# Expert weights in pages of 8 KB a partition, a contraction order to match, and a last normalization with two-row products

## The chip, the cores and the metric

The kernel runs on one core of a Trainium2 chip. The metric is the device time of one execution in microseconds (us), from the first to the last instruction and what the runtime lays around them. The engines have names of their own in the profile: PE is TensorE (its weight loads stand apart as PEld), DVE is VectorE, ACT is ScalarE, POOL is GpSimd, and SP is SyncE, which here issues nearly all transfers.

## What is computed

One block of a diffusion transformer over 512 latent tokens of 1024 channels, with 256 context tokens. First an attention half (a latent attention of 8 heads beside a differential attention of 4), then an expert half, each followed by a residual and a layer norm. The change touches both halves, the second most:

```python
def ec_moe(h, w_router, b_router, w1, w3, w2):
    cap = EC_CAPACITY * n // N_EXPERTS                       # 64 tokens an expert
    aff = softmax((h @ w_router + b_router), axis=-1)
    g, idx = top_k(swapaxes(aff, 1, 2), cap)                 # each of 16 experts takes 64 tokens
    xe = h[bidx, idx]
    hid = silu(einsum('becd,edf->becf', xe, w1)) * einsum('becd,edf->becf', xe, w3)
    ye = einsum('becf,efd->becd', hid, w2) * g[..., None]
    return zeros_like(h).at[bidx, idx].add(ye)

x = layer_norm(ALPHA * x + g2 * ec_moe(x * (1 + sc2) + sh2, ...), ln2_g, ln2_b)
```

Each expert has three matrices of 1024 x 1024 in float32, 12.6 MB; sixteen experts are 201 MB.

## The kernel before

Tokens lie on 128 partitions in NT = 4 tiles. The attention half multiplies the tokens with w_in in blocks of columns. Each block has four pieces of weights: a piece is loaded raw (`w_load`, L192), split into a high and a low part (`w_piece`, L198; ACT makes the high part, DVE the low one), and multiplied in three products (`mm3`, L79). The pages for that are the N_WS = 6 buffers of `wpage` (L128), 4 KB a partition each. Beside these products run the sums over w_ada (`mod_chunk`, L334), whose loads share SP's queue. The same small pages hold a part of the softmax (L758) and the weights of the branch outputs (`wo_load`, L789); the output projection has pages of its own (`page`, N_PG = 18, and `page2`, N_PG2 = 9).

The expert half works on pairs of experts (the loop at L1232). For a pair it gathers the tokens by products with one-hot matrices (`gather`, L1122), multiplies with w1 and w3 (`up_`, L1164), transposes (`hid_t`, L1179), multiplies with w2 (`down`, L1185), and puts the result back into the accumulators `acc` by one-hot products (`scatter`, L1193), half of it inside the next pair's `up_`. PE's instructions run in the written order there (`manual_schedule`, L1228).

The weights come through a ring of pages. `order` (L920) lists all pieces of 128 rows in the order of use; `prefetch` (L947) issues them on SP, each into the next of N_RING = 36 pages (L928), and SP waits there until the page is free. Nine pieces (`places`, L926) go into tiles that are not in use yet (`hold`, L944). A piece is 512 KB: 128 partitions with one row of 4 KB each. The contraction index of partition p in piece k is 128 k + p, and the activations that meet the weights are cut in the same way.

At the end the last pair's w2 is taken in three parts of columns (PARTS, L40: first column, width, rows in a page). `put` (L1278) scales and splits a part's product at once, and the function that it returns puts it back and takes statistics; that one is called after the first piece of the next part (L1310). The last part is accumulated in PSUM (`fin`). After it come the mean and variance, and for each tile two DVE passes over 768 columns (L1335, L1336); ACT and POOL do the last 256 columns (L1325 to L1331). The rows ln2_g and ln2_b are loaded as broadcasts behind the last weights (L1265).

## Time and profile before

| | |
|---|---|
| median of 3 runs | 1049.84 us (1048.28 to 1052.63) |
| the profiled execution | 1047.56 us |
| its span, first to last instruction | 1045.8 us |
| PE busy | 977.7 us, 93% of the span |
| PEld, DVE, ACT, POOL busy | 614.1, 451.9, 278.2, 176.1 us |
| moved by DMA | 266.97 MB, mean 255 GB/s |
| the chain that ended last | PE 72%, DMA 16%, DVE 7% |

The profile shows one execution. Busy shares are means over stages with different limits, so the stages are read one by one: the span cut into 40 slices, tables of stretches with the busy time of each engine, the granted clock of TensorE (1.00 is 2.4 GHz, 0.50 is 1.2 GHz), the share of time in which the 16 DMA engines had packets, and what they moved; then lists of who waited for whom; then the chain of work that ended last. A line number such as L1174 is that of the kernel's source.

### The profile page before, as it was taken

What the parts mean: (1) busy time and instruction counts of PE and PEld (TensorE: products, weight loads), DVE (VectorE), ACT (ScalarE), POOL (GpSimd) and SP (SyncE); (2) the same over time, 40 slices, a digit from 0 to 9 for tenths busy, and PEclk for the clock granted to TensorE, in tenths of its full rate; (3) what the DMA queues carried; (4) which work ended last, traced back from release to release, by engine and by line L of the source; (5) the groups of instructions that cost most, each with busy time, mean ns of one, the idle gap of its engine ahead of it and who ended that gap; (6) DMA issues with size and microseconds to landing.
All of it is one profiled execution on the core that took longest, in us unless ns stands there. A gap on an engine that the chain in (4) does not pass through costs nothing.

```text
span 1045.8 us, 13799 instructions
## 1 busy us (share of the span) xinstructions
PE 977.7 (93%) x5266; PEld 614.1 (59%) x5266; DVE 451.9 (43%) x870; ACT 278.2 (27%) x556; POOL 176.1 (17%) x177
## 2 busy tenths in 40 slices
PE   6999998989999999999986999999999999999992
PEld 5888976768778777777754443535353534334331
DVE  2382365753678556648473512221313131111227
ACT  1222324224777555544120101010101010010010
POOL 2340020202577422210020500000000000000004
PEclk9999999999999999999997999999999999999996
DMA  9944347763012000028948979999999999999993
GB/s 297 290 152 136 97 115 247 232 201 82 21 39 58 22 19 22 21 82 295 411 167 321 371 300 409 409 409 409 409 410 409 408 410 407 410 409 409 409 372 115
DMA packets 101209, 266.97 MB, mean 255 GB/s; under 512 B 14020, under 2 KB 37528, under 8 KB 101144
## 3 DMA queue, kind: packets, MB, share of 16 engines
q1 hardware_dynamic: 100248, 264.52, 68.3%
q0 software_dynamic: 320, 1.05, 0.4%
q8 instruction: 41, 0.67, 0.3%
q10 hardware_dynamic: 576, 0.52, 0.1%
q14 instruction: 24, 0.20, 0.1%
HBM read 261.47 MB, written 2.10 MB: 252 GB/s over the span
## 4 chain that ended last, share of the span: by engine, by line
PE 72%; DMA 16%; DVE 7%; ACT 2%; issue 2%; POOL 2%; SPq 0%; DVEq 0%; ACTq 0%; POOLq 0%
PE h L1174 16%; DMA wr<-moe_w 10%; PE y L1190 9%; PE mx L1137 6%; PE acc L83 5%; PE acc L82 5%; PE acc L81 5%; PE sc L652 4%; PE tpb L660 3%; DMA wa<-w_ada 3%; PE av L840 3%; PE mx L1203 2%; DMA wraw<-w_in 2%; PE tp L236 2%; PE po L83 1%
## 5 line engine op out<-in xcount | busy, mean ns | idle before, releaser
L1174 PE MATMUL h<-wr,xe 128*64 128x512 f32 x1024 | 233.6, 598 | 8.7 <-DMA wr<-moe_w 7.2
L1174 PEld LDWEIGHTS h<-wr,xe 128*64 128x64 f32 x1024 | 68.3, 136 | 162.9 <-issue 106.6
L1190 PE MATMUL y<-wr,hidT 128*64 128x512 f32 x448 | 97.7, 594 | 0.0
L641 DVE TENSOR_REDUCE nm<-sc 128x1 f32<-128x768 f32 x64 | 61.0, 953 | 34.3 <-PE sc L652 33.8
L1177 DVE TENSOR_TENSOR hid<-hid,h 128x512 f32<-128x512 f32 x16 | 11.0, 687 | 145.2 <-PE h L1174 145.2
L1149 POOL TENSOR_TENSOR oh<-oh,aff 128x512 f32<-128x512 f32 x8 | 8.4, 1048 | 352.8 <-PE mx L1137 352.8
L1190 PEld LDWEIGHTS y<-wr,hidT 128*64 128x64 f32 x448 | 31.5, 137 | 61.8 <-issue 58.1
L642 ACT ACTIVATE P<-sc,nm 128x768 f32<-128x768 f32 x64 | 57.6, 901 | 31.8 <-DVE nm L641 22.7
L1137 PE MATMUL mx<-oh,xn 128*128 128x128 f32 x512 | 60.3, 279 | 1.4 <-DVE oh L1127 1.4
L1137 PEld LDWEIGHTS mx<-oh,xn 128*128 128x128 f32 x512 | 59.2, 196 | 2.5 <-issue 1.3
L74 ACT ACTIVATE whi<-wraw 128x1024 fp32r<-128x1024 f32 (+1 forms) x32 | 33.5, 1046 | 99.4 <-DMA wraw<-w_in 75.4
L77 DVE TENSOR_TENSOR wlo<-wraw,whi 128x1024 fp32r<-128x1024 f32 (+1 forms) x32 | 39.2, 1227 | 45.2 <-PE acc L82 29.7
L74 ACT ACTIVATE ye<-y 128x512 fp32r<-128x512 f32 (+2 forms) x17 | 9.7, 572 | 178.8 <-DVE y L1197 98.7
L81 PE MATMUL acc<-xlh,whi 128*128 128x512 f32 x128 | 51.5, 402 | 2.1 <-ACT whi L74 2.1
L1204 DVE TENSOR_TENSOR acc<-acc,mx 128x512 f32<-128x512 f32 x56 | 34.7, 680 | 41.4 <-PE mx L1203 41.4
L1176 ACT ACTIVATE hid<-h 128x512 f32<-128x512 f32 x16 | 9.6, 597 | 155.6 <-PE h L1174 155.6
L82 PE MATMUL acc<-xll,whi 128*128 128x512 f32 x128 | 50.7, 396 | 0.0
L83 PE MATMUL acc<-xlh,wlo 128*128 128x512 f32 x128 | 50.2, 401 | 0.3 <-DVE wlo L77 0.3
L81 PE MATMUL acc<-whi,xlh 128*128 128x512 f32 (+1 forms) x128 | 49.6, 391 | 1.0 <-ACT whi L74 1.0
L1197 DVE SCALAR_TENSOR_TENSOR y<-y,gate,g2b 128x512 f32<-128x512 f32 x14 | 9.9, 754 | 92.5 <-PE y L1190 92.5
L83 PE MATMUL acc<-whi,xll 128*128 128x512 f32 (+1 forms) x128 | 48.7, 381 | 0.5 <-POOL xll L77 0.5
L82 PE MATMUL acc<-wlo,xlh 128*128 128x512 f32 (+1 forms) x128 | 48.8, 381 | 0.2 <-DVE wlo L77 0.2
(339 smaller groups left out, 1707.3 us busy)
## 6 DMA issues: line engine op xcount, KB each, us to landing
wr<-moe_w SPq DMA_DIRECT2D x372, 512.0 KB, 10.2
wa<-w_ada SPq DMA_DIRECT2D x32, 512.0 KB, 4.3
wraw<-w_in SPq DMA_DIRECT2D x28, 512.0 KB, 5.2
wa<-w_ada SPq DMA_DIRECT2D x8, 1024.0 KB, 9.4
wr<-moe_w SPq DMA_DIRECT2D x16, 384.0 KB, 8.5
outraw<-w_out SPq DMA_DIRECT2D x8, 512.0 KB, 9.6
xq<-x SPq DMA_DIRECT2D x4, 512.0 KB, 8.2
q<-q SPq DMA_DIRECT2D x16, 128.0 KB, 2.3
```

The source lines that it names most:

```text
L74: S.activation(hi, src, AF.Copy)
L77: (eng_lo or V).tensor_tensor(lo, src, f(hi), op=OP.subtract)
L81: T.matmul(ps, lh, rh, start=start, stop=False)
L82: T.matmul(ps, lh, rl, start=False, stop=False)
L83: T.matmul(ps, ll, rh, start=False, stop=stop)
L641: V.tensor_reduce(nm, ps[:, :768], axis=AX.X, op=OP.max, negate=True)
L642: S.activation(p, ps[:, :768], AF.Exp, bias=nm, accum_out=z)
L652: T.matmul(ps[:, a:b], l, r[:, a:b], start=i == 0, stop=i == len(passes) - 1)
L1137: T.matmul(pss[hf][:, kk * 128:(kk + 1) * 128], xn[t][:, k * 128:(k + 1) * 128], o[:, t].rearrange("p e s -> p (e s)"), start=t == 0, stop ...
L1174: T.matmul(ph[i][64 * hf:64 * hf + 64, :], xe[:, k, sl], w[:, hf * 512:(hf + 1) * 512], start=k == 0, stop=k == KD - 1)
L1190: T.matmul(py[hf][r0:r0 + 64, :], hT[:, e % 2, fc % 4, fc // 4, :], w[:, hf * 512:(hf + 1) * 512], start=fc == 0, stop=fc == KD - 1)
L1204: V.tensor_tensor(acc[t][:, hs], acc[t][:, hs], ps, op=OP.add)
```

## The change

Pages are 8 KB a partition, [128, 2, 1024], and half as many: 3, 9, 4 and 2. The contraction index of the experts is cut as (k p i) with i of two: partition p holds rows 256 k + 2 p and 256 k + 2 p + 1 of a matrix, which follow one another in HBM, and a transfer is 1 MB. What meets these weights takes every second column (`chan`): the gather's xn, the transposes of hid and of xn, and the vectors and router weights that belong to channels. In the attention half a page holds two raw pieces (`halves_`) or a high and a low part. The held pieces are pairs of halves of four pages.

At the end, `put` is called whole as soon as a part's product is there. Parts 0 and 1 are multiplied by ln2_g then (part 0 on DVE, part 1 on POOL). After the statistics, minus mean over deviation and a row of ones are transposed into two rows, and a product of these with the two rows ln2_g, ln2_b gives the term that a single DVE pass adds. The rows of ln2 are loaded on ACT's queue at the end of the last but one pair, into xn.

Left out below are the same edits in `rows_use`, `latent`, `mod_end` and `page`.

```diff
-N_WS, N_PG, N_PG2, N_PG3, N_P, N_WA = 6, 18, 9, 3, 5, 3
+N_WS, N_PG, N_PG2, N_PG3, N_P, N_WA = 3, 9, 4, 2, 5, 3
...
-PARTS = (0, 384, 2), (384, 384, 2), (768, 256, 4)
+PARTS = (0, 384, 4), (384, 384, 4), (768, 256, 8)
...
-    def wpage(name, dt=F32, shape=None):
-        return ws.tile(shape or [128, 2, 512], dt, name=name, tag="ws", bufs=N_WS)
+    def wpage(name, dt=F32):
+        return ws.tile([128, 2, D], dt, name=name, tag="ws", bufs=N_WS)
+    pairs = {}
+    def halves_(key, page_, name, dt=F32):
+        if key in pairs:
+            return pairs.pop(key)[:, 1]
+        pairs[key] = page_(name, dt)
+        return pairs[key][:, 0]
+    def chan(k):
+        return slice(256 * (k // 2) + k % 2, 256 * (k // 2) + 256, 2)
...
         if (col, kk) not in raws:
-            raws[col, kk] = wpage("wraw")
+            raws[col, kk] = halves_("wraw", wpage, "wraw").rearrange("p (k n) -> p k n", k=2)
             dma(raws[col, kk][:, :, :n], w_in[:, 2 * kk:2 * kk + 2, col:col + n])
...
         raw = w_load(col, n, kk)
-        hi = wpage("whi", F32R)
-        lo = wpage("wlo", F32R)
+        hi, lo = (wpage_[:, i].rearrange("p (k n) -> p k n", k=2) for wpage_ in (wpage("whl", F32R),) for i in range(2))
         split(hi[:, :, :n], lo[:, :, :n], raw[:, :, :n])
...
-    dma(wrt, A["moe_w_router"][0].rearrange("(k p) e -> p k e", p=128))
+    dma(wrt.rearrange("p (k i) e -> p k i e", i=2), A["moe_w_router"][0].rearrange("(k p i) e -> p k i e", p=128, i=2))
...
-                                       wpage("P1", F32, [128, D])[:, :768] if m else p_tile()))
+                                       halves_("P1", wpage, "P1")[:, :768] if m else p_tile()))
...
-        raw = page_("oraw", F32, [128, 4, 256])
+        raw = halves_("oraw", page_, "oraw").rearrange("p (k n) -> p k n", k=4)
...
-        hi = page_("ohi", F32R, [128, 4, 256])
-        lo = page_("olo", F32R, [128, 4, 256])
-        split(hi, lo, raw)
-        return hi, lo
+        hl = page_("ohl", F32R).rearrange("p i (k n) -> p i k n", k=4)
+        split(hl[:, 0], hl[:, 1], raw)
+        return hl[:, 0], hl[:, 1]
...
-        raw = page("outraw", F32, [128, 2, 512])
+        raw = halves_("outraw", page, "outraw").rearrange("p (k n) -> p k n", k=2)
...
-        woh[hf].append(page_("woh", F32R, [128, 2, 512]))
-        wol[hf].append(page_("wol", F32R, [128, 2, 512]))
+        hl = page_("wohl", F32R).rearrange("p i (k n) -> p i k n", k=2)
+        woh[hf].append(hl[:, 0])
+        wol[hf].append(hl[:, 1])
...
-    def page2(name, dt=F32, shape=None):
-        return Q2.tile(shape or [128, D], dt, name=name, tag="pg2", bufs=N_PG2)
-    wsrc = {n: A["moe_" + n][0].rearrange("e (k p) n -> e p k n", p=128) for n in ("w1", "w3", "w2")}
+    def page2(name, dt=F32):
+        return Q2.tile([128, 2, D], dt, name=name, tag="pg2", bufs=N_PG2)
+    wsrc = {n: A["moe_" + n][0].rearrange("e (k p i) n -> e p k i n", p=128, i=2) for n in ("w1", "w3", "w2")}
...
-             for k in range(KD) for n in ns]
-    order[-2 * KD:] = [(E_N - 2 + i, "w2", (q, kh)) for q, p in enumerate(PARTS) for kh in range(KD // p[2]) for i in range(2)]
+             for k in range(KD // 2) for n in ns]
+    order[-KD:] = [(E_N - 2 + i, "w2", (q, kh)) for q, p in enumerate(PARTS) for kh in range(KD // p[2]) for i in range(2)]
...
-    places = {2: "gb", 5: "ye", 8: "acc0", 10: "acc1", 12: "acc2", 13: "hid", 16: "acc3", 21: "ohT", 27: "hidT"}
+    places = {2: ("gb", "acc0"), 8: ("acc1", "acc2"), 10: ("acc3", "ye"), 12: ("ohT", "hidT")}
...
             c0, w, ks = PARTS[q]
-            dma(t[:, :ks * w].rearrange("p (k n) -> p k n", k=ks), wsrc[nm][e, :, ks * kh:ks * kh + ks, c0:c0 + w])
-        else:
-            dma(t, wsrc[nm][e, :, k, :])
-        loaded[e, nm, k] = t
+            t = t.rearrange("p i d -> p (i d)")[:, :ks * w].rearrange("p (k i n) -> p k i n", i=2, n=w)
+            for a in range(ks // 2):
+                dma(t[:, a], wsrc[nm][e, :, ks // 2 * kh + a, :, c0:c0 + w])
+            loaded[e, nm, k] = t
+            return
+        dma(t, wsrc[nm][e, :, k])
+        for j in range(2):
+            loaded[e, nm, 2 * k + j] = t[:, j]
...
     def hold(nm):
-        load(next(i for i in places if places[i] == nm), place(nm).tile([128, D], F32, name="wr", tag=nm, bufs=1))
+        i, j = next((i, j) for i in places for j in range(2) if places[i][j] == nm)
+        e, n, k = order[i]
+        t = place(nm).tile([128, D], F32, name="wr", tag=nm, bufs=1)
+        dma(t, wsrc[n][e, :, k, j])
+        loaded[e, n, 2 * k + j] = t
...
-            load(order_r[r], page_("wr", F32, [128, D]))
+            load(order_r[r], page_("wr"))
...
-                T.transpose(ps[:, k * 128:(k + 1) * 128], xn[t][:, (4 * hf + k) * 128:(4 * hf + k + 1) * 128], ident)
+                T.transpose(ps[:, k * 128:(k + 1) * 128], xn[t][:, chan(4 * hf + k)], ident)
...
-    def page3(name, dt=F32, shape=None):
-        return rM2.tile(shape or [128, D], dt, name=name, tag="pg3", bufs=N_PG3)
+    def page3(name, dt=F32):
+        return rM2.tile([128, 2, D], dt, name=name, tag="pg3", bufs=N_PG3)
...
-    for nm in ("ye", "hid", "ohT", "hidT"):
+    for nm in ("ye", "ohT", "hidT"):
...
-                T.matmul(pss[hf][:, kk * 128:(kk + 1) * 128], xn[t][:, k * 128:(k + 1) * 128],
+                T.matmul(pss[hf][:, kk * 128:(kk + 1) * 128], xn[t][:, chan(k)],
...
-            T.transpose(ps[:, j * 128:(j + 1) * 128], hid[:, i, j * 128:(j + 1) * 128], ident)
+            T.transpose(ps[:, j * 128:(j + 1) * 128], hid[:, i, chan(j)], ident)
...
         waiting = py, ohT, gt
+        if pr == E_N // 2 - 2:
+
+            lng, lnb, gbr = xn[1], xn[2], xn[0][0:2]
+            for i, nm in enumerate(("ln2_g", "ln2_b")):
+                S.dma_start(xn[1 + i], A[nm].to_broadcast([128, D]))
+                S.dma_start(xn[0][i:i + 1], A[nm])
     prefetch(len(order_r))
-    ln2 = []
-    for nm, place in (("ln2_g", "xe"), ("ln2_b", "hid")):
-        b = me.tile([128, D], F32, name="ln2", tag=place, bufs=1)
-        dma(b, A[nm].to_broadcast([128, D]))
-        ln2.append(b)
-    lng, lnb = ln2
     nb = D // BN_W
...
                     V.bn_stats(bs[:, t, (c0 + b) // BN_W, :], r[:, b:b + BN_W])
+                if not last:
+                    (G if q else V).tensor_tensor(r, r, lng[:, qs_], op=OP.mult)
         return rest
-    rest = None
+    mrs = me.tile([128, NT, 2], F32, name="mrs")
+    V.memset(mrs[:, :, 1], 1.0)
     for q, (c0, w, ks) in enumerate(PARTS):
...
         for kh in range(KD // ks):
-            wp = [piece(E_N - 2 + i, "w2", (q, kh))[:, :ks * w].rearrange("p (k n) -> p k n", k=ks) for i in range(2)]
+            wp = [piece(E_N - 2 + i, "w2", (q, kh)) for i in range(2)]
             for kk in range(ks):
...
                 for i in range(2):
-                    T.matmul(py[64 * i:64 * i + 64, :w], hT[:, i, fc % 4, fc // 4, :], wp[i][:, kk, :],
+                    T.matmul(py[64 * i:64 * i + 64, :w], hT[:, i, fc % 4, fc // 4, :], wp[i][:, kk // 2, kk % 2, :],
                              start=fc == 0, stop=fc == KD - 1)
-            if rest:
-                rest()
-                rest = None
-        rest = put(q, py)
-    rest()
-    order_.close()
+        put(q, py)()
     ov = out[0].rearrange("(t p) d -> p t d", p=128)
     mv = me.tile([128, NT, 2], F32, name="mv2")
-    rs2 = me.tile([128, 2, NT], F32, name="rs2")
+    rs2 = me.tile([128, NT], F32, name="rs2")
     for t in range(NT):
         V.bn_aggr(mv[:, t, :], bs[:, t])
-    G.tensor_scalar(rs2[:, 0, :], mv[:, :, 1], 1.0, EPS / ALPHA ** 2, op0=OP.mult, op1=OP.add)
-    G.tensor_tensor(rs2[:, 0, :], rs2[:, 0, :], negh[:, :NT], op=OP.pow)
-    V.scalar_tensor_tensor(rs2[:, 1, :], mv[:, :, 0], -1.0, rs2[:, 0, :], op0=OP.mult, op1=OP.mult)
+    V.tensor_scalar(rs2, mv[:, :, 1], EPS / ALPHA ** 2, None, op0=OP.add)
+    G.tensor_tensor(rs2, rs2, negh[:, :NT], op=OP.pow)
+    V.scalar_tensor_tensor(mrs[:, :, 0], mv[:, :, 0], -1.0, rs2, op0=OP.mult, op1=OP.mult)
+
+    mt = psd.tile([128, 512], F32, name="mx", bufs=3)
     for t in range(NT):
-        S.activation(acc[t][:, c0:], fin[t], AF.Identity, scale=rs2[:, 0, t:t + 1], bias=rs2[:, 1, t:t + 1])
-    done = []
+        T.transpose(mt[0:2, t * 128:(t + 1) * 128], mrs[:, t, :], ident)
+    mr = me.tile([2, 512], F32, name="mr", tag="hid", bufs=1)
+    V.tensor_copy(mr, mt[0:2])
+
+    for t in range(NT):
+        S.activation(acc[t][:, c0:], fin[t], AF.Identity, scale=rs2[:, t:t + 1], bias=mrs[:, t, 0:1])
+        G.tensor_tensor(acc[t][:, c0:], acc[t][:, c0:], lng[:, c0:], op=OP.mult)
+        G.tensor_tensor(acc[t][:, c0:], acc[t][:, c0:], lnb[:, c0:], op=OP.add)
+        S.dma_start(ov[:, t, c0:], acc[t][:, c0:])
     for t in range(NT):
         o = acc[t]
-        G.tensor_tensor(o[:, c0:], o[:, c0:], lng[:, c0:], op=OP.mult)
-        G.tensor_tensor(o[:, c0:], o[:, c0:], lnb[:, c0:], op=OP.add)
-        S.dma_start(ov[:, t, c0:], o[:, c0:])
-        parts = [slice(0, c0)] if t < NT - 1 else [slice(0, c0 // 2), slice(c0 // 2, c0)]
-        for p in parts:
-            with tc.issue_after(done[-1].ins) if t > 1 else nullcontext():
-                V.scalar_tensor_tensor(o[:, p], o[:, p], mv[:, t, 0:1], lng[:, p], op0=OP.subtract, op1=OP.mult)
-            done.append(V.scalar_tensor_tensor(o[:, p], o[:, p], rs2[:, 0, t:t + 1], lnb[:, p], op0=OP.mult, op1=OP.add))
-            dma(ov[:, t, p], o[:, p])
+        for a, b in ((0, 512), (512, c0)):
+            w = psd.tile([128, 512], F32, name="y" if a else "mx", bufs=2 if a else 3)
+            T.matmul(w[:, :b - a], mr[:, t * 128:(t + 1) * 128], gbr[:, a:b], start=True, stop=True)
+            V.scalar_tensor_tensor(o[:, a:b], o[:, a:b], rs2[:, t:t + 1], w[:, :b - a], op0=OP.mult, op1=OP.add)
+            if t == NT - 1:
+                dma(ov[:, t, a:b], o[:, a:b])
+        if t < NT - 1:
+            dma(ov[:, t, :c0], o[:, :c0])
+    order_.close()
```

## Rows read from the trace of the kernel before

**Rows 1.** The page, part 2: 40 slices of the span, busy tenths and GB/s.

```profile
PE   6999998989999999999986999999999999999992
...
GB/s 297 290 152 136 97 115 247 232 201 82 21 39 58 22 19 22 21 82 295 411 167 321 371 300 409 409 409 409 409 410 409 408 410 407 410 409 409 409 372 115
```

**Rows 2.** Stretches: length, busy us of each engine, PEclk, DMA share, GB/s.

```profile
613.00:865.00 252.00, 252.00 (x1288) 110.63 (x1284) 61.79 (x116) 28.35 (x57) 4.20 (x4) 1.00 1.03 408
865.00:1000.00 135.00, 127.36 (x611) 48.30 (x608) 25.58 (x49) 11.00 (x21) 2.10 (x2) 1.00 1.03 408
1000.00:1012.00 12.00, 11.33 (x59) 5.73 (x57) 2.23 (x5) 1.69 (x3) 0.00 (x0) 1.00 1.06 372
1015.00:1018.00 3.00, 2.86 (x16) 1.05 (x12) 1.39 (x5) 0.00 (x0) 0.00 (x0) 1.00 1.10 351
600.00:613.00 13.00, 13.00 (x83) 8.15 (x84) 2.73 (x8) 2.17 (x4) 1.05 (x1) 1.00 0.57 205
```

**Rows 3.** Waits from 865 to 1000 us: total us, times, longest.

```profile
PEld h L1174 <- DMA wr<-moe_w: 43.8, 47, 1.1
```

**Rows 4.** The chain in order of time: start us, us, what.

```profile
662.48 13.88 PE y L1190 x64
...
709.67 7.15 PE mx L1137 x64
717.25 13.88 PE y L1190 x64
```

**Rows 5.** Queues and DMA issues: packets, MB, share; KB each, us to landing.

```profile
q8 instruction: 41, 0.67, 0.3%
...
wr<-moe_w SPq DMA_DIRECT2D x372, 512.0 KB, 10.2
...
ln<-ln_g SPq DMA_DIRECT2D x1, 512.0 KB, 8.7
```

**Rows 6.** The tile wraw: duration ns min/median/max, and us from issue to landing.

```profile
L74 ACT ACTIVATE whi<-wraw x32: 897/1060/1325, 15.9 to 253.0; 128x1024 fp32r<-128x1024 f32 x28, 128x832 fp32r<-128x832 f32 x4
L77 DVE TENSOR_TENSOR wlo<-wraw,whi x32: 1017/1224/1829, 17.5 to 254.4; 128x1024 fp32r<-128x1024 f32 x28, 128x832 fp32r<-128x832 f32 x4
...
DMA to landing us min/median/max: 3.4/4.8/8.7
```

**Rows 7.** Stretches of ten us in the projections, columns as in rows 2.

```profile
170.00:180.00 10.00, 7.09 (x26) 4.16 (x25) 5.45 (x6) 6.45 (x28) 0.00 (x0) 0.83 0.61 196
...
210.00:220.00 10.00, 7.88 (x27) 5.78 (x25) 4.99 (x4) 2.57 (x3) 0.00 (x0) 0.83 0.69 226
```

**Rows 8.** Groups by line, 600 to 1000 us: busy us, mean ns, idle.

```profile
L1137 PE MATMUL mx<-oh,xn 128*128 128x128 f32 x433 | 49.5, 275 | 0.0
L1137 PEld LDWEIGHTS mx<-oh,xn 128*128 128x128 f32 x432 | 48.8, 192 | 0.0
...
L1197 DVE SCALAR_TENSOR_TENSOR y<-y,gate,g2b 128x512 f32<-128x512 f32 x14 | 9.9, 754 | 92.5 <-PE y L1190 92.5
...
L117 PE MATMUL mx<-rm,one 1*128 1x512 f32 x4 | 1.9, 639 | 0.0
```

**Rows 9.** The chain from 1010 us on: start us, us, what.

```profile
1009.41 9.24 DMA wr<-moe_w
...
1018.70 1.94 PE y L1308 x14
...
1025.50 0.40 DVE y L1283
...
1030.04 0.83 POOL rs L1321
...
1032.11 1.01 DVE acc L1335
...
1041.72 0.96 DVE acc L1336
```

**Rows 10.** Two us of the end, columns as in rows 2.

```profile
1030.00:1032.00 2.00, 0.00 (x0) 0.00 (x0) 0.81 (x1) 0.00 (x0) 1.87 (x2) 0.50 0.00 0
```

More of the change, by code (lines that the diff above doesn't have):

```diff
@@ L168, in _layer @@
     V.tensor_scalar(cs[:, :, 1], sg[:, 8:16], 0.5, None, op0=OP.mult)
-    rows = st.tile([68, 128], F32, name="rows")
+    rows = st.tile([52, 128], F32, name="rows")
+    lnr = st.tile([128, 512], F32, name="xtmp", bufs=3)[:8, :256]
     def rows_load():
@@ L175, in rows_load @@
         dma(rows[51:52], A["diff_g_subln"])
-        dma(rows[52:60], A["ln1_g"][0].rearrange("(k p) -> k p", p=128))
-        dma(rows[60:68], A["ln1_b"][0].rearrange("(k p) -> k p", p=128))
+        for i, nm in enumerate(("ln1_g", "ln1_b")):
+            dma(lnr[4 * i:4 * i + 4], A[nm][0].rearrange("(k p) -> k p", p=256))
     def rows_use():
         tp = psa.tile([128, 512], F32, name="tp", bufs=2)
-        T.transpose(tp[:, :68], rows, ident[:68, :68])
-        V.tensor_copy(vecs[:, 16:84], tp[:, :68])
+        T.transpose(tp[:, :52], rows, ident[:52, :52])
+        for k in range(2):
+            T.transpose(tp[:, 64 + 8 * k:72 + 8 * k], lnr[:, k::2], ident[:8, :8])
+        V.tensor_copy(vecs[:, 16:68], tp[:, :52])
+        for k in range(2):
+            V.tensor_copy(vecs[:, 68 + k:84:2], tp[:, 64 + 8 * k:72 + 8 * k])
         V.tensor_scalar(gsub, vecs[:, 67:68], 1.0 - LAMBDA_INIT, None, op0=OP.mult)
@@ L463, in latent @@
             dma(tq[:, :, i, :], A[nm].rearrange("(t p) d -> p t d", p=128))
-        wukv = wpage("wukv", F32, [128, HEADS, 128])
+        wukv = halves_("wu", wpage, "wu").rearrange("p (h d) -> p h d", d=128)
         dma(wukv, A["mla_w_ukv"][0].rearrange("p (h d) -> p h d", d=128))
@@ L468, in latent @@
         for k in range(2):
-            wuq = wpage("wuq", F32, [128, D])[:, :768]
+            wuq = halves_("wu", wpage, "wu")[:, :768]
             dma(wuq, A["mla_w_uq"][0, k * 128:(k + 1) * 128, :])
@@ L587, in mod_end @@
             for c in range(4):
-                T.transpose(pt[:, c * 128:(c + 1) * 128], rm[i][:, c * 128:(c + 1) * 128], ident)
+                T.transpose(pt[:, c * 128:(c + 1) * 128], rm[i][:, chan(c)], ident)
             ptr.append(pt.rearrange("p (c g o) -> p g c o", g=4, o=32))
@@ L868, in _layer, with page @@
     Q, _ = pool("pages", side="left")
-    def page(name, dt=F32, shape=None):
-        return Q.tile(shape or [128, D], dt, name=name, tag="pg", bufs=N_PG)
+    def page(name, dt=F32):
+        return Q.tile([128, 2, D], dt, name=name, tag="pg", bufs=N_PG)
     yp, close_yp = pool("yp", side="left")
```

## Prediction

> **What bounds the kernel now.** I read the 40 slices first, then tables of stretches, then the waits, the chain in order of time, and the groups by line. In the slices [rows 1] the reader is to see two halves. Up to some 450 us PE is busy and DMA, after the first slices, is not full. From the 25th slice to the 38th, GB/s stands at 407 to 410, whatever PE does. The table [rows 2] says why: 408 GB/s both from 613 to 865 us, where PE never rests, and from 865 to 1000, where it does. So in the expert half the stream of weights runs flat out from 613 us on, and PE catches up with it. The waits [rows 3] show PE on the stream's heels after 865: 47 weight loads waited for a page. The chain [rows 4] gives PE's own pace: 717.25 - 662.48 = 54.8 us a pair of experts. A pair is 48 transfers of 512 KB = 25.2 MB, at 408.5 GB/s 61.6 us. The stream is the slower by 6.8 us a pair; the pages filled beforehand hide that until 865. Just before 613 the ring of pages was full: 205 GB/s from 600 to 613 [rows 2], with PE in the gather and releasing no page. What happens there is set by PE, and what follows by the stream. So three things count: the stream's rate after 613 us, what is put into the stream, and the end behind it. All before 613 counts only where PE stalls.
>
> **The rate.** The same table has three sizes of contiguous row at a full queue [rows 2]: 4 KB rows (613 to 1000) 408, in the slices 409, taken as 408.5 GB/s, 1.5 KB rows (parts of w2, 1000 to 1012) 372, 1 KB rows (1015 to 1018) 351. Over 16 engines that is 160.4, 66.1 and 46.7 ns a row. The line through the first two is 9.5 ns + 0.0368 ns a byte; it gives 47.2 for 1 KB, measured 46.7, so it is a line. An 8 KB row would take 9.5 + 301.8 = 311 ns: 421 GB/s, 3.0% more. In the new layout one partition's two rows of a weight matrix lie one behind the other both in HBM and in the page, so 8 KB can go as one. The trace has no 8 KB row of weights. The bounds are therefore nothing (cut back into 4 KB) and the line. Packets above 4 KB do exist: queue q8 moved 0.67 MB in 41, 16 KB each [rows 5]. I take the line: 387 us x (1 - 408.5/421) = **-11.5 us**, with 0 as the other end. The Trainium skill (DMA: Bandwidth & Descriptors, Why small descriptors are slow) speaks against so much: it has a fixed cost of about 3 cycles a packet, one cycle for each 32 bytes. The rows make it 9.5 ns against 1.18 ns for 32 bytes, some 8. By the page's figure 4 KB to 8 KB would be worth 1.1%, an estimate of -4.4 us; the measured line decides for the sum, and the smaller gain is a rival below.
>
> **What is put into the stream.** Both ln2 rows (512 KB each) used to be issued behind the last weights [rows 5], so they delayed nothing on the path. Now ACT issues them when the last gather has read xn, near 940 us, into the full stream: 1.05 MB / 0.42 = **+2.5 us** (none, if the stream had slack there; rows 1 show none). The two 4 KB rows for the products are nothing beside that.
>
> **Pages of 8 KB.** 36 ring pages of 4 KB become 18 of 8 KB, so as much is filled beforehand. A page is free only when both its halves are used: after the full ring the first release comes one half later, 13.88/16 = **+0.9 us** [rows 4]. Transfers in flight: 10.2 us to landing [rows 5] at 1.28 us each is 8; eight of 1 MB hold more pages, but the bytes landed by a given time, which PE lives on, are the same. The pieces held in other tiles now belong to early, paired halves; PE did not wait there before, so I give nothing.
>
> **The projections.** Six small pages become three, with two raw weights in one page and hi and lo in another. Raw piece 2 of a block can now be loaded only when piece 1 is split, not piece 0. SP issues in order, so the w_ada transfers behind it wait too, and VectorE's sums over them. From the tile's rows [rows 6]: split 1.06 + 1.22, landing 4.8 (worst 8.7), split again 2.3: 9.4 us, against two pieces of 24 matmuls, some 11 us. The slack is 1.6 us; at the worst landing 2.3 us are missing. PE already stalls in two stretches here, 2.9 and 2.1 us idle in ten [rows 7]. Six blocks of this length: 0 to +14 us, and as piece 3 is issued earlier than now, a gain of up to 2 is possible. Landings were near the median, so I take **+1.5 us**.
>
> **Strided loads.** Gather, hid and xn transposes now load weights from every second column. PE's loads take 192 ns and overlap the matmuls, 7.15 us a gather of 64 [rows 4, 8]. No row shows a stationary operand at a step of two. Bounds: nothing, or twice the time (+7.2 us a gather). I take nothing, since the words used are 8 bytes apart; the rival has the price. The Trainium skill (Advanced Engine Details and Errata, Memory Cachelines) wants two hits in a 16-byte line for full speed, and a step of two float32 gives two; no run so far shows it.
>
> **The end.** The last w2 transfer landed about 1018.65 + 2 x 1.49 = 1021.6 us [rows 2, 9]; call it D. Before, part 1 was put back only after half of part 2's product (1020.6 on), and VectorE came to part 2 at 1025.50, D + 3.9. Now part 1 is put back when ready, but PE, in written order, waits for VectorE and ACT (about 1.8 us) and then spends 2.3 on the put, as before, and part 2's product (2 x 1.94) comes after: D + 3.2, so -0.7. The first part's multiplication by gamma (four of 0.5 us) falls between parts; part 1's goes to POOL, idle there. POOL's 0.83 us [rows 9] becomes a small VectorE one: -0.8. Then the old end is two VectorE passes over 768 columns a tile, 1032.11 to 1042.68 = 10.6 us. The new one: transposes 0.8, copy 0.65, then for each tile a two-row product of 512 and of 256 columns, each followed by one VectorE pass (0.75 for 512 columns [rows 8], some 0.45 for 256). A 512-column product of one row took 0.94 us (two instructions, 1.9 for two products) at full clock [rows 8]; the clock here stands at 0.50, that is 1.2 GHz [rows 10], so 1.9. Warm 4 x 1.4 = 5.6, cold 11.3, so 7.5 to 13.2 us with the last pass: -3.1 to +2.6. PE may come warm half way; I take -0.3. Sum for the end **-1.8** (-4.6 to +1.1). The last output transfer stays, 3.1 us.
>
> **Sum.** -11.5 + 2.5 + 0.9 + 1.5 - 1.8 = -8.4 us. The profiled execution took 1047.56 (span 1045.8), so 1039.2 on its scale; the three runs shown have a median of 1049.84, 2.3 above it, and on that scale I forecast **1041.4 us**.
>
> **The rivals.**
> - *The rate stays at 409* (rows cut at 4 KB, or engines at their limit). For it: the share of 1.03 is already called full. Against it: the line through three sizes. -8.4 + 11.5 = +3.1: 1053. Chance 0.13.
> - *Only part of the 9.5 ns is paid per row*, the rest per 4 KB. With a third of it per row, 8 KB takes 2 x 160.4 - 3.2 = 317.6 ns, 412.7 GB/s, -3.9 us instead of -11.5: 1049. For it: no row here is longer than 4 KB. Against: the line holds from 1 to 4 KB. Chance 0.07. The Trainium skill's rule above would come out here.
> - *Slower: strided weight loads.* PE's slack under the faster stream is small: its work without waits ends part 2 at some 1009 us (pair 6's product at 936.5 + 13.9, then 33 of up, 3, 14 of parts and 8 of puts), the stream's at 1016. So from 7 us / (7 x 72 loads) = 14 ns a load, PE becomes the bound. At twice the time: 7.2 for the first gather, 7 x 7.8 for the others, less 7: 1041 + 55 = 1096. For it: no cover in the gather, PE and its loads are both full there [rows 8]. Against: nothing seen. Chance 0.07.
> - *The three pages stall the projections* by the worst landing each time: +14 in place of 1.5: 1053.6. For it: two stretches stall already [rows 7]. Against: DMA has room there, landings were mostly short. Chance 0.08.
>
> **How the numbers follow.** The forecast has 0.65. Half a per cent, 5.2 us, is about what a measurement of this kernel tells from no change. Of the 0.65 I give 0.62 to faster, 0.03 to within 0.5%. Smaller gain: within. Rate unchanged: 0.12 within, 0.01 slower. Pages: 0.04 and 0.04. Strides: 0.07 slower; 0.02 more for slower from the sum of small costs is taken from the within. Faster 0.62, within 0.24, slower 0.14. The likeliest case's own range is 1034 (warm products, no stall) to 1046; for 8 in 10 it goes up to the unchanged rate, 1034 to 1053.
>
> **What would show it.** Right: packets of 8 KB, 420 GB/s or more from 613 us on, the last weights near 1013, PE waiting for pages later than 865 (near 950); the table of the projections no more than 2 us longer before 470; after the last weights some 22 us in place of 24. Wrong: 409 GB/s again with 8 KB pages (rate); weight loads above 200 ns in the gather and a pair longer than 54.8 us (strides); more idle PE from 150 to 240 us with SP waiting for VectorE's split (pages); products at 1.9 us each to the end (clock).

## The result and the profile after

| | median of the runs, us | ratio to before, 95% interval | profiled run: time, span, us |
| --- | --- | --- | --- |
| before | 1049.1 (1045.2 to 1052.6, 6 runs) | 1 | 1047.6, 1045.8 |
| changed | 1056.5 (1055.4 to 1058.6, 6 runs) | 1.0077 [1.0056, 1.0098] | 1055.8, 1053.9 |

The changed kernel is 7.4 us slower; the forecast was 1041.4. Yet the rate of the stream of weights, the term that carried the forecast, came out as worked out. One execution of the run on the places (1419 us) and one of the run on the deferred puts (4803 us) were in a slow state and are in no figure below. The page of the changed kernel, GB/s in 40 slices, answers to [rows 1]:

```profile
GB/s 301 253 174 155 82 125 255 242 187 61 28 33 56 40 1 41 1 160 294 325 152 312 318 284 422 421 421 421 421 421 421 421 420 420 422 421 420 415 286 80
DMA packets 74827, 266.95 MB, mean 253 GB/s; under 512 B 10686, under 2 KB 34058, under 8 KB 51724
```

From the 25th slice on 421 GB/s, where [rows 1] has 409: 311 ns for 8 KB on one of 16 engines, as the line through three row sizes gave. By an estimate from the fixed cost a packet in the Trainium skill (DMA: Bandwidth & Descriptors, Why small descriptors are slow), 1.1% would have come of it. Measured is 2.9%, and the measurement decides.

Stretches of the changed kernel, columns as in [rows 2]:

```profile
613.00:865.00 252.00, 252.00 (x1284) 113.31 (x1285) 58.74 (x112) 27.09 (x53) 7.46 (x7) 1.00 0.98 407
865.00:1000.00 135.00, 129.29 (x650) 56.13 (x646) 29.87 (x56) 13.44 (x27) 2.10 (x2) 1.00 1.01 420
...
700.00:1030.00 330.00, 318.97 (x1624) 143.69 (x1622) 82.56 (x172) 34.29 (x68) 8.12 (x8) 0.99 0.99 406
```

and the last of these for the kernel before:

```profile
700.00:1030.00 330.00, 316.75 (x1600) 135.09 (x1596) 79.66 (x175) 31.65 (x62) 5.25 (x5) 1.00 1.00 396
```

The first row shows where the gain went. From 613 to 865 the mean is 407 GB/s, as before, though the stream runs at 421 once it is full: it became full later. At 700 us the changed kernel had 330 x 406 = 134.0 MB still to move, the one before 330 x 396 = 130.7. The 3.3 MB are 7.8 us of stream at 421, and the rate saves 9.5 us on 130.7 MB (130.7 / 0.4085 less 130.7 / 0.421). Most of the delay stands between the first gather and the first pair's product with w2. In the rows, oh are the one-hot matrices, xe the gathered tokens, which VectorE scales and takes out of PSUM (the evacuation), h the products with w1 and w3, y those with w2. PE in the changed kernel (start us, us, what, and in brackets the idle time before it with its releaser; of y only the start is read, as the window ends there):

```profile
576.66 4.04 PE L1163 MATMUL mx<-oh,xn 128*128 128x128 f32 x32
583.81 20.82 PE L1200 MATMUL h<-wr,xe 128*64 128x512 f32 x96 [3.11 <-DVE xe L1168]
...
606.59 0.74 PE L1163 MATMUL mx<-oh,xn 128*128 128x128 f32 x4 [0.90 <-DVE oh L1153]
608.00 7.33 PE L1163 MATMUL mx<-oh,xn 128*128 128x128 f32 x60 [0.67 <-DVE oh L1153]
...
617.53 0.65 PE L1216 MATMUL y<-wr,hidT 128*64 128x512 f32 x2
```

The same of the kernel before:

```profile
571.70 3.84 PE L1137 MATMUL mx<-oh,xn 128*128 128x128 f32 x32
576.04 20.82 PE L1174 MATMUL h<-wr,xe 128*64 128x512 f32 x96 [0.50 <-DVE xe L1142]
...
607.64 0.65 PE L1190 MATMUL y<-wr,hidT 128*64 128x512 f32 x2
```

The first gather started at 562.57 (before 558.92), the first y at 617.53 (607.64): of 9.9 us, 6.2 arose in between. PE waited 3.11 us for VectorE's evacuation of the gather (xe; before 0.50) and 1.57 us for the next one-hot (before 0.17); 1.3 more lie in the first half of the gather, 6.50 in place of 5.18 us, as the clock rose from 0.50 to 1.00 only near 568 us and not near 561. VectorE at that time, in the changed kernel:

```profile
581.49 0.90 DVE L1242 TENSOR_TENSOR acc<-xn,gb 128x512 f32<-128x512 f32 x1 [10.94 <-PE mx L1163]
582.74 0.69 DVE L1243 TENSOR_TENSOR acc<-acc,gb 128x512 f32<-128x512 f32 x1 [0.36 <-DMA gb<-ln_b]
583.35 1.36 DVE L1168 TENSOR_SCALAR xe<-mx,ghv,bhv 128x128 f32<-128x128 f32 x4
...
605.36 2.59 DVE L1153 TENSOR_TENSOR oh<-iot,slt 128x256 f32<-128x256 f32 x2
```

and in the kernel before:

```profile
575.58 1.37 DVE L1142 TENSOR_SCALAR xe<-mx,ghv,bhv 128x128 f32<-128x128 f32 x4 [9.99 <-PE mx L1137]
577.16 0.69 DVE L1216 TENSOR_TENSOR acc<-xn,gb 128x512 f32<-128x512 f32 x1 [0.22 <-PE h L1174]
...
597.58 0.75 DVE L1127 TENSOR_TENSOR oh<-iot,slt 128x256 f32<-128x256 f32 x2
```

Two instructions of the base sum (`base`: xn times gamma, plus beta) stand ahead of the evacuation that PE waits for. The row blames PE's gather, but that was done at 576.66 + 4.04 = 580.70. The rows of the tile gb, the gamma and beta of the base sum, point to another: POOL issued the load of gamma at 574.8, and the shortest landing is 6.6 us, so it was there at 581.4 at the earliest (worked out, as the trace gives no landing of this one load):

```profile
L1238 POOL DMA_DIRECT2D gb<-ln_g x2: 587/672/757, 574.8 to 597.2; - x2
...
DMA to landing us min/median/max: 6.6/7.4/9.4
```

Before, the issues were at 568.1 and 570.4, with landings as long (6.7 to 9.0). The tiles that the base sum needs hold weights first. gb held w1's second piece and now the third; ye held a piece of the first expert and now one of the second, so the gamma of POOL's half of the base sum is loaded at 597.2 in place of some 570. And in the program before, the planner (which orders each engine's instructions) had put all eight evacuations ahead of the base sum on VectorE.

The one-hot was late for another reason. POOL worked on its half from 604.99 on (before from 578.59 to 591.29), and VectorE's two one-hot instructions beside it took 2.59 us in place of 0.75. So it is in all traces: 2.25 to 2.90 us in the eight with the places of the changed kernel, where POOL's half runs beside them, 0.75 or 0.76 in the other eight, where it was done before.

At the other end, the chain of the changed kernel from the last w1 and w3 on:

```profile
1001.83 2.82 PE h L1200 x12
...
1007.96 5.33 PE y L1337 x32
...
1013.99 0.04 issue
1014.03 0.50 ACT ye L74
1014.56 0.57 DVE ye L77
...
1017.34 5.33 PE y L1337 x32
...
1025.92 1.65 PE mx L1317 x4
1027.57 4.32 PE y L1337 x32
1031.92 0.50 DVE y L1309
...
1036.74 1.05 POOL rs L1346
...
1039.82 2.07 PE mx L1364 x2
1041.89 0.85 PE y L1364 x2
1042.74 1.71 PE mx L1364 x2
```

From 1007.96 on no transfer of weights stands in the chain: PE, not the stream, ends the three parts. It is VectorE's turn for part 2 at 1031.92, where [rows 9] has 1025.50. From the end of the last h product to the end of the span it is 1053.9 - 1004.6 = 49.3 us; before 1045.8 - 999.7 = 46.1 (the last h started at 998.65 and took 1.08). The granted clock in that stretch, columns as in [rows 10]:

```profile
1024.00:1026.00 2.00, 1.32 (x5) 0.74 (x5) 1.24 (x3) 0.19 (x1) 0.00 (x0) 0.88 0.01 4
1026.00:1028.00 2.00, 2.00 (x8) 1.37 (x10) 2.00 (x9) 0.00 (x0) 1.00 (x2) 0.50 0.00 0
...
1040.00:1042.00 2.00, 2.00 (x3) 0.96 (x4) 0.07 (x1) 0.00 (x0) 1.92 (x4) 0.50 0.20 66
1048.00:1050.00 2.00, 2.00 (x4) 0.66 (x2) 0.77 (x2) 0.00 (x0) 0.00 (x0) 0.50 0.43 165
```

It was at 0.50 (1.2 of 2.4 GHz) within the second put, after PE had stood still 1.59 us for ACT. It rose to 1.00 in part 2's product, was at 0.50 again by 1036, while PE stood still for 3.54 us, and stayed there through all two-row products, with PE busy 10.00 us of 10.00 from 1040 to 1050.

### The profile page after: what moved, and what is told of

Same layout as the page of the kernel before. It is cut to its first block, busy times and chain, and to the rows that moved or that the text cites. A ratio compares the mean times of both kernels' runs of the same rounds, so it can differ in the third digit from the quotient of the medians.

```text
span 1053.9 us, 13455 instructions
## 1 busy us (share of the span) xinstructions
PE 989.2 (94%) x5288; PEld 630.4 (60%) x5288; DVE 443.7 (42%) x877; ACT 277.6 (26%) x556; POOL 174.1 (17%) x180
## 4 chain that ended last, share of the span: by engine, by line
PE 73%; DMA 13%; DVE 6%; issue 4%; ACT 2%; POOL 2%; SPq 0%; ACTq 0%; DVEq 0%; POOLq 0%
PE h L1200 16%; PE y L1216 8%; DMA wr<-moe_w 7%; PE mx L1163 5%; PE sc L670 5%; PE acc L83 4%; PE acc L82 4%; PE acc L81 4%; DMA wa<-w_ada 3%; PE tpb L678 3%; PE av L857 3%; PE mx L1229 2%; PE tp L254 1%; PE y L1337 1%; PE av L794 1%
## 5 line engine op out<-in xcount | busy, mean ns | idle before, releaser
L1200 PE MATMUL h<-wr,xe 128*64 128x512 f32 x1024 | 226.1, 594 | 10.7 <-DMA wr<-moe_w 7.1
L1200 PEld LDWEIGHTS h<-wr,xe 128*64 128x64 f32 x1024 | 71.4, 137 | 154.4 <-issue 130.8
L1163 PE MATMUL mx<-oh,xn 128*128 128x128 f32 x512 | 64.8, 289 | 2.8 <-DVE oh L1153 2.8
L1163 PEld LDWEIGHTS mx<-oh,xn 128*128 128x128 f32 x512 | 63.7, 204 | 4.1 <-DVE oh L1153 1.9
L77 DVE TENSOR_TENSOR whl<-wraw,whl 128x1024 fp32r<-128x1024 f32 (+1 forms) x32 | 39.2, 1226 | 56.0 <-ACT whl L74 56.0
L74 ACT ACTIVATE whl<-wraw 128x1024 fp32r<-128x1024 f32 (+1 forms) x32 | 33.2, 1038 | 107.4 <-DMA wraw<-w_in 57.3
L81 PE MATMUL acc<-xlh,whl 128*128 128x512 f32 x128 | 51.0, 399 | 0.0
L83 PE MATMUL acc<-xlh,whl 128*128 128x512 f32 x128 | 50.2, 396 | 0.5 <-DVE whl L77 0.5
L81 PE MATMUL acc<-whl,xlh 128*128 128x512 f32 (+1 forms) x128 | 49.5, 391 | 1.0 <-ACT whl L74 1.0
L82 PE MATMUL acc<-xll,whl 128*128 128x512 f32 x128 | 50.4, 394 | 0.0
L83 PE MATMUL acc<-whl,xll 128*128 128x512 f32 (+1 forms) x128 | 48.7, 381 | 0.5 <-POOL xll L77 0.5
L82 PE MATMUL acc<-whl,xlh 128*128 128x512 f32 (+1 forms) x128 | 48.7, 381 | 0.2 <-DVE whl L77 0.2
```

What stands on the lines that cost most here:

```text
L74: S.activation(hi, src, AF.Copy)
L77: (eng_lo or V).tensor_tensor(lo, src, f(hi), op=OP.subtract)
L81: T.matmul(ps, lh, rh, start=start, stop=False)
L82: T.matmul(ps, lh, rl, start=False, stop=False)
L83: T.matmul(ps, ll, rh, start=False, stop=stop)
L1163: T.matmul(pss[hf][:, kk * 128:(kk + 1) * 128], xn[t][:, chan(k)], o[:, t].rearrange("p e s -> p (e s)"), start=t == 0, stop=t == NT - 1)
```

## The experiments

All times are medians; "ratio" is to the kernel before, run on the same chip. In the cuts of the edits `...` marks what is left out.

**The whole old end** on the changed kernel.

```diff
-        put(q, py)()
+                if rest and fc == KD // 2 - 1:
+                    rest()
+                    rest = None
+        rest = put(q, py)
...
-            T.matmul(w[:, :b - a], mr[:, t * 128:(t + 1) * 128], gbr[:, a:b], start=True, stop=True)
+                V.scalar_tensor_tensor(o[:, p], o[:, p], mv[:, t, 0:1], lng[:, p], op0=OP.subtract, op1=OP.mult)
```

> The changed kernel with the end of before: each part put back after half of the next product, the ln2 rows issued behind the last weights, two VectorE passes at the end. Theory (the end costs about 8 us, and 2.5 us more lies in the stream through the ln2 rows; the front's losses eat the rate's gain): 1056.5 - 8 - 2 = about 1046 to 1047, that is 2 to 3 us faster than before. Rival (the end is as good as before, all is lost ahead of it): within 2 us of the changed kernel, 1055 or more. Last VectorE pass some 21 us behind the last weights in place of 29.

1049.6 us, ratio 1.0002 [0.9987, 1.0018]. PE in its trace:

```profile
1014.11 3.23 PE L1333 MATMUL y<-wr,hidT 128*64 128x384 f32 x18
1017.96 1.94 PE L1333 MATMUL y<-wr,hidT 128*64 128x256 f32 x14 [0.62 <-DMA wr<-moe_w]
1019.83 0.98 PE L1316 MATMUL mx<-ye,ohT 128*128 128x384 f32 x4
...
1022.11 1.95 PE L1333 MATMUL y<-wr,hidT 128*64 128x256 f32 x16
```

Part 2's product waits for the stream again, and part 1's put lies inside it. The new end, with the ln2 rows in the stream, costs the changed kernel 6.9 us.

**The new end alone**, on the kernel before with its 4 KB pages and PARTS.

```diff
-            if rest:
-                rest()
-                rest = None
-        rest = put(q, py)
+        put(q, py)()
...
+            T.matmul(w[:, :b - a], mr[:, t * 128:(t + 1) * 128], gbr[:, a:b], start=True, stop=True)
```

> The kernel before with only the new end (parts put back at once, gamma between parts, two-row products, ln2 rows issued by ACT into the stream); pages and layout as before. Theory: PE waits twice for VectorE and ACT, the products stay at the clock 0.50, and the ln2 rows cost 2.5 us: 1049.1 + 7 to 10 = 1056 to 1059. Prediction's term for it: -1.8 + 2.5 = 1049.8. Rival (the end only costs because PE comes late behind a faster stream): within 2 us of before.

1057.0 us, 1.0076 [1.0047, 1.0106]: 7.9 us (8.0 by the ratio), about the same as from the other side, with pages and front as before.

**The places**: the tiles of the base sum hold earlier weights.

```diff
-    places = {2: ("gb", "acc0"), 8: ("acc1", "acc2"), 10: ("acc3", "ye"), 12: ("ohT", "hidT")}
+    places = {2: ("gb", "acc0"), 5: ("ye", "acc1"), 7: ("acc2", "acc3"), 12: ("ohT", "hidT")}
```

> The changed kernel, with the tiles that the base sum needs (ye, and three accumulators) holding weights of the first expert in place of the second, so that they are free some 6 us earlier. Theory (the late base sum keeps VectorE from the next gather's evacuation and one-hot, which set back the start of the flat-out stream by some 5 us): the product of the first pair starts 3 to 5 us earlier (near 613 to 614 in place of 617.6), the whole 3 to 5 us faster, 1052 to 1053. Rival (the stream or the end decides alone): within 1 us of the changed kernel.

1058.3 us, 1.0089 [1.0062, 1.0117]: nothing gained. In its trace the wait for the one-hot is gone, as POOL's half of the base sum is over by then (the one-hots take 0.76 us), but PE still waits 3.16 us for xe. For that wait the theory had named the wrong cause: not when the tiles come free, but the place in VectorE's queue, which the runs further down try.

**Without strides** (the weights stay in the new order).

```diff
-        return slice(256 * (k // 2) + k % 2, 256 * (k // 2) + 256, 2)
+        return slice(128 * k, 128 * k + 128)
```

> The changed kernel, but the transposes of xn and hid and the gather take 128 neighbouring columns in place of every second one; the weights stay in the new order, so rows and weights no longer belong together. Theory (strided loads cost some 0.4 us a gather, 1.3 us in the first cold one, 0.1 us a transposition of hid): the first gather half 5.2 in place of 6.5 us, the others 7.15 in place of 7.54; the whole 2 to 3 us faster as long as PE is not ahead of the stream, 1053.5 to 1055. Rival (strides cost nothing, the slower gather is something else): no change in the gather, 1056.

1056.0 us, 1.0072 [1.0049, 1.0096]: nothing. Groups by line from 600 to 1000 us, the changed kernel and below it this one:

```profile
L1163 PE MATMUL mx<-oh,xn 128*128 128x128 f32 x448 | 54.3, 282 | 1.6 <-DVE oh L1153 1.6
L1163 PEld LDWEIGHTS mx<-oh,xn 128*128 128x128 f32 x448 | 53.5, 197 | 1.9 <-DVE oh L1153 1.9
```

```profile
L1163 PE MATMUL mx<-oh,xn 128*128 128x128 f32 x448 | 51.5, 275 | 1.4 <-DVE oh L1153 1.4
L1163 PEld LDWEIGHTS mx<-oh,xn 128*128 128x128 f32 x448 | 50.6, 192 | 1.8 <-DVE oh L1153 1.8
```

A load at a step of two costs 5 ns more, 0.4 us a gather (7.71 against 7.31 us), and the whole shows nothing of it. The first gather half took 6.40 us here and 5.58 to 6.50 us in the runs with strides, so its length is not theirs; the granted clock, 0.50 from 560 to 565 us in the changed kernel, fits it.

**Deferred puts, products kept**: half of the new end, the ln2 rows still in the stream.

```diff
-        put(q, py)()
+                if rest and fc == KD // 2 - 1:
+                    rest()
+                    rest = None
+        rest = put(q, py)
```

> The changed kernel, but each part is put back after half of the next part's product, as before; the two-row products, the gamma multiplications between the parts and the ln2 rows in the stream stay. Theory (of the 7 us that the old end gave back, most is PE's standing still in the two puts): 1056.5 - 4.5 = 1051 to 1053. Rival (the products at the low clock and the ln2 rows are the loss): 1055 or more.

1053.9 us, 1.0051 [1.0034, 1.0067]. The clock stays at 1.00 to the last put; the products still run at 0.50.

**Puts at once, two passes**: the other half.

```diff
-            T.matmul(w[:, :b - a], mr[:, t * 128:(t + 1) * 128], gbr[:, a:b], start=True, stop=True)
-            V.scalar_tensor_tensor(o[:, a:b], o[:, a:b], rs2[:, t:t + 1], w[:, :b - a], op0=OP.mult, op1=OP.add)
...
+                V.scalar_tensor_tensor(o[:, p], o[:, p], mv[:, t, 0:1], lng[:, p], op0=OP.subtract, op1=OP.mult)
+            done.append(V.scalar_tensor_tensor(o[:, p], o[:, p], rs2[:, 0, t:t + 1], lnb[:, p], op0=OP.mult, op1=OP.add))
```

> The changed kernel with parts put back at once, but mean and bias applied as before by two VectorE passes with the ln2 rows (still loaded by ACT into the stream); no gamma between the parts. Theory (products cost 2.5 us more than the passes they replace): 1056.5 - 2.5 = 1053 to 1055; with the run above and the run with the whole old end (1049.6) the two halves should add up. Rival (products as good as the passes): 1056 or more.

1057.4 us, 1.0079 [1.0052, 1.0105]: no gain. In its trace the passes do end 1.7 us sooner behind the last statistics (13.7 against 15.4 us), but the clock fell already at the end of the first put, part 1's product took 6.91 in place of 5.38 us, and that is about as much as the passes gave. So the expectation missed. The sum that it asked for left out the ln2 rows, which these two runs kept in the stream: 2.6 for the deferred puts, -0.9 for the passes and 3.9 for the rows (the run on them stands below) make 5.6 of the 6.9 us, the same within the noise.

**4 KB rows** on the run with the old end: each page by two transfers.

```diff
-        dma(t, wsrc[nm][e, :, k])
+        for j in range(2):
+            dma(t[:, j], wsrc[nm][e, :, k, j])
```

> As the run with the old end, but each page of 8 KB a partition is loaded by two transfers of 4 KB rows; all else the same. Theory (8 KB rows are worth 421 against 409 GB/s and the faster stream is what keeps that run level with before): 408 to 410 GB/s from 700 us on, some 11 us less of gain over 380 us, minus the 2 to 3 us that PE stands behind the stream there: 1057 to 1060. Rival (the rate no longer counts, PE's late start decides): within 2 us of 1049.6.

1064.2 us, 1.0157 [1.0133, 1.0180]: 409 GB/s from 700 on, and 14.6 us slower than with 8 KB rows. The rate is real, and worth more than the forecast had it.

**The base sum behind the evacuation** (old end, places as above; `xev` holds VectorE's evacuations of the first gather).

```diff
+                with tc.issue_after(xev[KD - 1].ins):
                     eng.tensor_tensor(acc[t][:, hs], xn[t][:, hs], gb[hf][:, 0], op=OP.mult)
...
```

> As the run with the old end, with VectorE's part of the base sum queued behind the evacuation of the second gather half, as it stood in the kernel before, and the tiles for the base sum holding weights of the first expert. Theory (the base sum ahead of the evacuation on VectorE kept PE from starting 4 to 5 us): no idle stretch of 3 us before the first pair's second half; from the start of the first gather to the first pair's product 50 us in place of 55.8; the whole 3 to 5 us faster than that run: 1045 to 1047, the best so far. Rival (the stream is the bound again and gives nothing): 1049 to 1050.

1043.4 us, 0.9951 [0.9934, 0.9968]: the fastest here, 5.7 us ahead of the kernel before. PE in its trace:

```profile
575.01 4.04 PE L1165 MATMUL mx<-oh,xn 128*128 128x128 f32 x32
579.55 20.82 PE L1202 MATMUL h<-wr,xe 128*64 128x512 f32 x96 [0.50 <-DVE xe L1170]
...
601.56 7.81 PE L1165 MATMUL mx<-oh,xn 128*128 128x128 f32 x64
...
611.57 0.65 PE L1218 MATMUL y<-wr,hidT 128*64 128x512 f32 x2
```

From the first gather (561.79) to y it is 49.8 us; in the run with the old end 55.8, before 48.7. So the first y starts 5.35 us earlier than in that run (616.92), and the last h product ends 4.3 us earlier (996.07 against 1000.37).

**The ln2 rows in the stream**, on the run with the old end.

```diff
+        if pr == E_N // 2 - 2:
+            for i, nm in enumerate(("ln2_g", "ln2_b")):
+                S.dma_start(xn[1 + i], A[nm].to_broadcast([128, D]))
...
-        dma(b, A[nm].to_broadcast([128, D]))
```

> As the run with the old end (1049.6), but ACT issues the two ln2 rows when the last gather has read xn, as in the changed kernel: one step moved, 1.05 MB put ahead of the last weights. Theory (they cost their own transfer time in a full stream): 1049.6 + 2.5 = 1052; with the products at the low clock (+1.8) this makes up the 1053.9 of the run with deferred puts and products. Rival (PE, not the stream, ends the last part there): 1049 to 1050.

1053.5 us, 1.0039 [1.0024, 1.0054]: 3.9 us for one moved step. With the three other runs that have these rows in the stream it makes a square: puts deferred, 1053.9 with products and 1053.5 with passes; puts at once, 1056.5 with products and 1057.4 with passes. Going at once costs 2.6 and 3.9 us; products or passes make no difference beyond the noise.

**The base sum behind the evacuation, new end kept**: the same edit on the changed kernel itself.

> The changed kernel with its new end, and only VectorE's part of the base sum put back behind the evacuation of the second gather half (with the tiles of the first expert, as in the fastest run so far). Theory (what the late first pair cost is independent of the end: the same 6 us as with the old end): 1056.5 - 6 = 1050 to 1051. Rival (the new end is bound by PE's own order, and gives part of it back): 1053 or more.

1051.5 us, 1.0021 [1.0008, 1.0034]: 5.0 us, about what it gave under the old end (6.2).

**TensorE kept busy**, on that run: `warm(n)` makes n products of 128 rows and 512 columns that nobody reads.

```diff
+        warm(1)
         put(q, py)()
+    warm(3)
```

> As the run before it (new end, base sum put back), and TensorE is given extra products whose results nobody reads: one of 512 columns ahead of each put, where it stands waiting for VectorE and ACT, and three behind the last put. Theory (the standing still lets the clock fall to 0.50 for the second put and for all of the two-row products, 2.56 us a tile): the granted clock stays at 1.00 to the first two-row product, that one takes 0.94 instead of 1.9 us, and the whole is 3 to 5 us faster than the run without them. Rival (the clock falls anyway, or two-row products don't hold it): the products take 1.9 us, the whole within 1 us or slower by the extra work.

1047.8 us, 0.9985 [0.9970, 1.0000]: 3.7 us faster for more work. From the end of the last h product to the end of the span its trace has 45.1 us, the run without the extra products 50.9. The two-row products in its trace, and then the stretches of two us over them (columns as in [rows 10]):

```profile
1036.58 1.12 PE L1374 MATMUL mx<-xn,mr 2*128 2x512 f32 x2 [0.77 <-DVE mr L1363]
...
1037.97 1.02 PE L1374 MATMUL mx<-xn,mr 2*128 2x512 f32 x2
...
1039.33 1.91 PE L1374 MATMUL mx<-xn,mr 2*128 2x512 f32 x2
```

```profile
1036.00:1038.00 2.00, 1.42 (x5) 0.87 (x6) 0.79 (x2) 0.72 (x2) 1.92 (x3) 1.00 0.00 0
1038.00:1040.00 2.00, 2.00 (x6) 1.05 (x5) 1.85 (x4) 0.00 (x0) 1.84 (x4) 0.80 0.30 104
1040.00:1042.00 2.00, 2.00 (x5) 1.11 (x4) 0.89 (x2) 0.56 (x1) 0.89 (x2) 0.50 1.01 387
```

The theory held for the puts (1.00 throughout) and for the first two tiles. Then the clock fell in the middle of the products, without a gap in PE's work there; PE had stood still 0.97 and 0.77 us shortly ahead of them.

**The order without the places**, old end.

> As the run with the old end, with VectorE's base sum queued behind the evacuation as in the fastest run (1043.4), but the tiles as the changed kernel has them (ye and three accumulators hold weights of the second expert). Theory (the queue order is what counts; the places alone gave nothing in the new end): 1044 to 1046. Rival (the late tiles delay the base sum all the same, then the next one-hot and gather): 1048 to 1050, with an idle stretch before the second gather.

1045.9 us, 0.9963 [0.9948, 0.9978]. The order alone gives 3.7 us. The places perhaps add the rest, 2.4 us (within the noise of two medians): POOL's half of the base sum runs beside the one-hots again, which take 2.25 us, and PE's waits for them, 0.56 and 0.67 us, are back.

**Two more on the fastest run**: without strides, and with 4 KB rows (edits as above).

> As the fastest run (old end, base sum behind the evacuation, 1043.4), with neighbouring columns in place of every second one in the gather and the transpositions; rows and weights then no longer belong together. Theory (0.4 us a gather lies on PE's path only up to the point where the stream takes over near 940 us, and the stream's start hangs on the first two gathers alone): 0 to 1.5 us faster. Rival (strides are the missing cost): 3 to 4 us faster, 1040.

1043.5 us, 0.9957 [0.9941, 0.9973]: the strides cost nothing that shows even with the front put right.

> As the fastest run, with each 8 KB page loaded by two transfers of 4 KB rows. Theory (rate worth 11.5 us in a stream that binds from 613 us to the end): 1043.4 + 11.5 = 1055, so that the rest of the change (pages of two halves, strides, attention pages) costs some 6 us against before. Rival (the rate was worth the 14.6 us seen with the late front): 1058.

1057.5 us, 1.0083 [1.0061, 1.0106]. The rate is again worth 14.1 us, so the rival held; and what is left of the change at equal rate, with the old end, costs 8.4 us.

## Why the prediction was wrong

The runs make a chain from before to the changed kernel, by medians. The middle steps are single edits (the third moves the tiles too); the first is all that is left of the change, the last has two halves:

| step | forecast, us | measured, us | between which runs |
| --- | --- | --- | --- |
| pages, strides, new parts of w2, at 4 KB rows | +2.4 | +8.4 | before to 4 KB rows on the fastest run |
| 8 KB rows | -11.5 | -14.1 | on to the fastest run |
| places, and base sum ahead of the evacuation | 0 | +6.2 | on to the old end |
| ln2 rows in the stream | +2.5 | +3.9 | on to the ln2 rows in the stream |
| puts at once and products | -1.8 | +3.0 | on to the changed kernel |
| sum | -8.4 | +7.4 | |

Each difference of two medians is uncertain by some 3 us (a ratio's interval here is 0.13 to 0.3% to each side). 15.8 us separate the sums.

*Rate: right.* 421 GB/s where the prediction wrote 421. Its worth is 14 rather than 11.5 us. In the traces of the two pairs, from the first y to the end of the last h product, 4 KB rows take 11.0 us (395.5 against 384.5) and 11.7 us (395.1 against 383.4) longer, as forecast. What the medians show beyond it lies ahead of that stretch or behind it, and is within the noise. The rivals "rate stays" and "only part" fell.

*Pages: the step that failed first.* The prediction gave nothing to the tiles that hold pieces, since "PE did not wait there before". It asked who waits for those pieces, and not who waits for those tiles: the base sum does, VectorE carries it in the planner's order, and PE waits behind VectorE. Two runs with order and places put right show 5.0 and 6.2 us, the order alone 3.7. It also leant on the pages filled beforehand to hide the front. They hide little of a late start: the stream is flat out from the point at which PE releases pages, and of the 5.35 us by which the fastest run has its first y earlier, 4.3 are left at the last h product.

*The rest of the first line, +6 beyond the forecast, is read and not tried.* Against before, the trace with 4 KB rows on the fastest run has 1.8 us more between gather and first y, and 3.4 us more from there to the end of the last h (which the prediction put at 0.9, for a page released only when both halves are used). Half of the 3.4 shows at the end of that stretch: behind its last wait for w1 and w3 PE has 12 instructions left (2.79 us) where before it had 4 (1.08), since a page of 1 MB is waited for whole. The prediction had such waits cost nothing, as "the bytes landed by a given time, which PE lives on, are the same". The rest of the 8.4, some 3 us, would have to lie ahead of the gather, where it can't be told from the scatter: all fourteen kernels with 8 KB pages start the gather at 561.0 to 566.5 us, the two with pages of before at 558.92 and 562.87. One piece stands in every trace in which the clock held there: from 340 to 350 us PE is busy 8.19 to 8.87 us with 8 KB pages, against 9.68 and 9.84 with those of before, where the weights of the output products share three pages with the softmax. These pages were not varied, so the cause of this part stays open.

*Projections and strides.* The projections end at 265.1 us against 265.3: the +1.5 is 0, and the rival of +14 fell (its time, 1041.4 + 14 - 1.5, is 1053.9 and not 1053.6). Strides at 0 were right: weight loads of 197 ns in place of 192, and nothing in the whole. The Trainium skill (Advanced Engine Details and Errata, Memory Cachelines) asks for two hits in a line for full speed; the trace agrees but for these 5 ns.

*The end.* The step that failed is "part 2's product (2 x 1.94) comes after: D + 3.2", D being the landing of the last w2 transfer. It took the stream to end part 2. With h late, PE came to part 0 at 1007.96 in place of 1002.90, and then had three products of 5.3, 5.3 and 4.3 us and two puts in a row, with ACT and VectorE waited for in each and the clock down to 0.50 in the second: VectorE came to part 2 at 1031.92, some 10 us behind D. D itself was about 1022, as before (75 GB/s from 1022 to 1024, before 113), where the prediction had 1013: the late start and the ln2 rows had used up what the rate gave. By the runs, deferring gives back 2.6 and 3.9 us (each uncertain by some 3) and keeping PE busy 3.7 (with warm products in it). For the products the prediction's cold bound came true: 2.56 us a tile, from minus mean over deviation (1037.82) to the end of the last pass (1050.94) 13.1 us, bounds 7.5 to 13.2; against the passes that is 0.4 us more by medians with the puts deferred, 0.9 less with the puts at once, and 1.8 more by the two traces with the puts deferred.

*The ln2 rows* cost 3.9 us by the runs and 2.5 by their bytes; the difference is within the measurement.

## What to carry to other kernels

Where a tile is lent to a weight first, ask who needs the tile next, not only who needs the weight, and look at the place of that work in its engine's queue: the one line that put it back was worth 3.7 us, with the places 5 to 6, against 14 of the faster stream. Here, where a stream bounds the kernel, a late start of it was paid nearly in full at its end (4.3 of 5.35 us), and so was 1 MB put into it (3.9 us). A step that "does it at once" on an engine with a written order made that engine stand still; filling the gap with the next product (2.6 and 3.9 us), or even with idle products (3.7), was faster than going early.
